# A hybrid decoder layer on one core: the second head pair's q and k are split ahead of the exponentials, and an open projection is closed within the scores

## The chip, the core and the metric

The kernel runs on one core of a Trainium2 chip as one launch. A time is the device time of one execution in microseconds (us); lower is better. Three executions of the kernel before were timed, and one more was taken by the hardware profiler. TensorE (PE in the profile) multiplies matrices, VectorE (DVE) and ScalarE (ACT) work on elements, GpSimd (POOL) does elementwise work and issues DMAs, and SyncE (SP) issues DMAs. Each engine runs its own instructions in the order in which they stand; semaphores hold an instruction until what it needs is done.

## The reference, cut to what matters

One layer on 512 tokens of width 1024, all in float32:

```python
proj = h @ w_in                       # [q | k | v | pool_in | gate_logits]
y_attn = moba_attention(q, k, v, rel_bias) @ w_branch_attn   # 8 heads of 64
y_pool = multiscale_pool(p, w_pool_group, pool_scale) @ w_branch_pool
mixed = gates[:, :, 0] * y_attn + gates[:, :, 1] * y_pool    # gates = sigmoid(g)
h = layer_norm(ALPHA * h + mixed @ w_out, ln1_g, ln1_b)
a, u = split(h @ w_ffn_in)            # 2816 columns each
f = (gelu(causal_dwconv(a)) * u) @ w_ffn_out
h = layer_norm(ALPHA * h + f, ln2_g, ln2_b)
```

With blocks of 256 keys, two blocks in all and up to three chosen, the attention is plain causal softmax attention with a bias by distance:

```python
logits = q @ k.T / 8 + bias[distance]     # masked to the past
p = softmax(logits); out = p @ v
```

## The kernel before, in words

**Precision and form.** Most operands are cut into a high and a low part (`split`, lines 72 to 78): ScalarE rounds the high part into a tile named `whi` or `xT_hi`, and VectorE subtracts to get the low part (`wlo`). A product is then three matmuls, high by high, high by low and low by high (`mm3`, line 245).

**Seven products.** A pair of 128-column weight tiles against 512 tokens is done as a 2 by 2 block product with seven block products in place of eight (`seven`, line 289). Its weight parts are named A, X, D and Y; a group of 12 matmuls 256 wide (`s_mm`) multiplies one half of a part. In order: A twice (banks `sa..` and `sc..`), X, Y (onto the `sa` bank), D (onto the `sb` bank), X's second half (onto `sa`), and last Y's second half (onto `sa`). That last group, with the copy behind it, isn't issued at once: `close` is put in the list `pending`, and `flush` (line 260), called inside the next `seven`, issues it. Between the groups stand small steps: ScalarE copies partial sums out (lines 285, 299, 301), VectorE adds (lines 303, 307, 308). Line 308 writes into the very bank onto which the closing group adds.

**The stages around the change.** v is projected first. Then come five `seven` calls (line 576): number 0 for the pool branch, numbers 1 to 4 for q and k of the four head pairs. In the order of the instructions the bank `sai_674` belongs to the second head pair, `sai_809` to the third, and `sai_999` (after the change: `sai_1011`) to the fourth. `heads_done` (line 523) copies the closed q to the tile `quad`; `split_heads` (line 439) scales and cuts k and q into `kh`, `kl`, `qh`, `ql`. These four tiles exist once (`bufs=1`), so a pair's split has to wait for the last score matmul of the pair before.

**Scores, softmax, PV.** `scores(p)` (line 534) multiplies q and k of the two heads of a pair, 64 rows each, side by side on the two halves of TensorE's rows, into banks `sc0_01`, `sc0_2`, `sc0_3` and so on, and then calls `softmax` per head: VectorE adds the bias strip and takes the maxima (line 561), ScalarE takes the exponentials with their sums (line 567, first of all with a table load), VectorE the reciprocals, GpSimd multiplies (line 572). `trans` (line 618) transposes the result with TensorE; ScalarE copies the first 512 columns of `PT`, VectorE the rest in two copies. `pv` (line 636) multiplies by v in four key blocks, the columns that ScalarE copied first.

**What sets the order.** A scheduler places the instructions of each engine by the order of the code, the dependencies and its own estimates; `issue_after` holds an instruction behind another, `keep_in_program_order` pins it on TensorE. In the code before, the second pair's `split_heads` (line 672) is held behind the maxima and the exponentials of the second head (`nms[1]`, `exps[1]`). The branch and gate weights come through three raw buffers (`wraw`, `araw`) issued by SP, and `weights` fetches up to `state["limit"]`.

Of the kernel before, what the change touches and what calls it, by code (L numbers as in the profile page):

```python
# [18 lines left out]
NT = S // P  # L19
H = 8  # L20
# [32 lines left out]
def layer_kernel(ctx: ExitStack, tc: tile.TileContext, xT, x, w_v, w_c, rel_bias, invcnt, w_group,  # L53
# [30 lines left out]
    at = {}  # L84
# [43 lines left out]
    state = {"next": 0, "limit": WO0 - 1}  # L128
# [310 lines left out]
    def split_heads(p, *behind):  # L439
        qh, ql, kh, kl = QK[p] = [av.tile([P, S], F32R, tag=t, name=f"{t}_{p}", bufs=1)  # L440
                                  for t in ("qh", "ql", "kh", "kl")]
        with ExitStack() as held:
            for ins in behind:
                held.enter_context(tc.issue_after(ins.ins))
            for hi, lo, raw, scale in ((kh, kl, raw_k[p], -1.0), (flip(qh), flip(ql), raw_q[p], DH ** -0.5)):
                nc.scalar.activation(hi, raw, AF.Copy, scale=scale)
                nc.vector.scalar_tensor_tensor(lo, raw, scale, hi.bitcast(F32), op0=ALU.mult, op1=ALU.subtract)
# [79 lines left out]
    Ps = {}  # L527
# [3 lines left out]
    copies = {}  # L531
    offs = [0, P, 3 * P, 6 * P]

    def scores(p):
        two = (2 * p, 2 * p + 1)
        dst = {}
        for h in two:
            if h + 2 < H:
                load_strip(h + 2)
            b01 = bank(f"sc{h}_01")  # L540
            dst[h] = [b01[:, :2 * P], b01[:, 2 * P:], bank(f"sc{h}_2")[:, :3 * P], bank(f"sc{h}_3")]
        qh, ql, kh, kl = QK[p]
        for i in range(NT):
            n = max(2, i + 1) * P
            q = slice(i * P, (i + 1) * P)
            for m, (a, b) in enumerate(((qh, kh), (qh, kl), (ql, kh))):
                for e, h in enumerate(two):
                    own = slice(e * DH, (e + 1) * DH)
                    ins = nc.tensor.matmul(dst[h][i], a[own, q], b[own, :n], start=m == 0, stop=m == 2)
                    if e or m or i:  # L550
                        tc.keep_in_program_order(ins)
        for h in two:
            softmax(h, dst[h])

    def softmax(h, dst):
        pp = aw.tile([P, 10 * P], F32, tag="pp", name=f"pp{h}")
        nm = aw.tile([P, NT], F32, tag="nm", name=f"nm{h}")
        rs = aw.tile([P, NT], F32, tag="rs", name=f"rs{h}")
        for i in range(NT):
            n = (i + 1) * P  # L560
            nc.vector.tensor_tensor_reduce(out=pp[:, offs[i]:offs[i] + n], in0=dst[i][:, :n],
                                           in1=strips[h][:, S - n:], scale=1.0, scalar=-3.0e38,
                                           op0=ALU.add, op1=ALU.max, accum_out=nm[:, i:i + 1])
        nms[h] = nc.vector.tensor_scalar(nm, nm, -1.0, None, op0=ALU.mult)
        for i in range(NT):
            n = (i + 1) * P
            exps[h] = nc.scalar.activation(pp[:, offs[i]:offs[i] + n], pp[:, offs[i]:offs[i] + n], AF.Exp,
                                           bias=nm[:, i:i + 1], accum_out=rs[:, i:i + 1])
        nc.vector.reciprocal(rs, rs)  # L569
        for i in range(NT):  # L570
            n = (i + 1) * P
            state["norm"] = nc.gpsimd.tensor_scalar(pp[:, offs[i]:offs[i] + n], pp[:, offs[i]:offs[i] + n], rs[:, i:i + 1], 1.0,  # L572
                                    op0=ALU.mult, op1=ALU.mult)
        Ps[h] = pp

    for n in range(1 + pairs):
        if n == 0:
            u, done = xr[1][:, 3, :], lambda ba, u: pool_sum(0, ba)
        else:
            u = raw_k[n - 1] = qraw[n - 1][:, S:]  # L580
            done = lambda ba, u, p=n - 1: heads_done(p, ba)
        seven(("i", n), (xT_hi, xT_lo), ti, xr[1][:, 2, n % 2 * 256:n % 2 * 256 + 256], u, done)
        if n == 0:
            behind_sum.close()
            pool_dif(PLAIN[0], state["Y"])
            pool_sum(PLAIN[1], second)
            with tc.issue_after(state["acc"].ins):
                write_table(table)
        elif n == 1:
            pool_out(PLAIN[0])  # L590
            pool_dif(PLAIN[1], state["add"])
            pool_dif(0, state["add"])
            pool_sum(1, xr[1][:, 3, :], -1.0)
            add1 = state["add"]
        elif n == 2:
            pool_out(PLAIN[1])
            pool_dif(1, add1)
            with tc.issue_after(state["acc"].ins):
                load_strip(0)
                load_strip(1)  # L600
            split_heads(0, state["add"], state["copy"])
        elif n == 3:
            pool_out(0)
            pool_out(1)
            pooling.close()
            aw = attn.enter_context(tc.tile_pool(name="aw", bufs=4, side="right", reuse_waits="tile"))
            scores(0)
    phase.close()
    keep = keepp.enter_context(tc.tile_pool(name="keep", bufs=1, reuse_waits="tile"))
    gates = keep.tile([P, H, S], F32, name="gates")  # L610
# [5 lines left out]
    toff = {0: 0, 1: S, 3: S + 3 * P, 2: 2 * S}  # L616

    def trans(h):
        pp = Ps[h]
        PT = ap.tile([P, 10 * P], F32, tag="PT", name=f"PT{h}")  # L620
        bk = [bank(f"tr{h}_{n}") for n in range(3)]
        for kb in (0, 1, 3, 2):
            o = toff[kb]
            for i in range(kb, NT):
                c = o + (i - kb) * P
                nc.tensor.transpose(bk[c // S][:, c % S:c % S + P], pp[:, offs[i] + kb * P:offs[i] + (kb + 1) * P],
                                    ident)
        one = nc.scalar.activation(PT[:, :S], flip(bk[0]), AF.Copy)
        with ExitStack() as held:
            if h + 2 < H:  # L630
                held.enter_context(tc.issue_after(nms[h + 2].ins))
            nc.vector.tensor_copy(PT[:, S:2 * S], flip(bk[1]))
            copies[h] = one, nc.vector.tensor_copy(PT[:, 2 * S:], flip(bk[2][:, :2 * P]))
        PTs[h] = PT

    def pv(p):
        b = bank(f"ob{p}")
        for kb in range(NT):
            n = (NT - kb) * P
            for e in (1, 0):  # L640
                h = 2 * p + e
                state["pv"] = nc.tensor.matmul(b[e * DH:(e + 1) * DH, kb * P:], vv[:, kb, h * DH:(h + 1) * DH],
                                 PTs[h][:, toff[kb]:toff[kb] + n], start=kb == 0, stop=kb == NT - 1)
        split(oT_hi[:, p, :], oT_lo[:, p, :], b)
        state["o"] = state["hi"], state["lo"]

# [22 lines left out]

    with tc.issue_after(exps[0].ins):  # L670
        flush()
    split_heads(1, nms[1], exps[1])
    for h in range(H):
        pair, late = divmod(h, 2)
        if not late and h + 2 < H:
            scores(pair + 1)
        if fill:
            state["limit"] = at["z", 0]
            in_tile(*fill.pop(0))
        elif h < H - 1:  # L680
            early_fetch(h, at["z", 0] + h // 2)
            early_branch(h - 2 * GSEVEN)
        with ExitStack() as held:
            if h and not late:
                pv(pair - 1)
                held.enter_context(tc.issue_after(state["pv"].ins))
            trans(h)
        if not late and h + 4 < H:
            split_heads(pair + 2, nms[h + 3], exps[h + 3])
        if h == 0:  # L690
            with tc.issue_after(nms[2].ins), tc.issue_after(exps[0].ins):
                for k in range(4):
                    split(zT_hi[:, k, :], zT_lo[:, k, :], zT[:, k, :])
            oT_hi = keepz.tile([P, 4, S], F32R, tag="zT", name="oT_hi")
        if h == 5:
            with tc.issue_after(state["norm"].ins):
                for n, (k, t) in enumerate(((k1, t1), (k1, t2), (k2, t1), (k2, t2))):
                    nc.gpsimd.dma_start(quads[n], xT[k.start * P:k.stop * P, t].rearrange("(k p) t -> p k t", p=P))
                homes["g", "X"], homes["g", "D"] = lambda f: gX, lambda f: gD
                for q in "XD":  # L700
                    coming[q].remove(("g", GSEVEN))
                    fetch_raw(("g", GSEVEN), q)
                    homes.pop(("g", q))
        if h == H - 1:
            early_fetch(h, at["o", 1])
            early_branch(h - 2 * GSEVEN)
            state["limit"] = WO0 - 1
# [14 lines left out]
    gx.tile([P, 256], F32, name="gx_gap")  # L722
    for n in parts[1:]:
        tg[n] = tuple(gx.tile([P, 4, 256], F32R, name=f"g{n}_{q}") for q in ("hi", "lo"))
    state["limit"] = WO0 - 1
    mts = {}

# [492 lines left out]
```

## Time and profile before

| what | value |
|---|---|
| median of three executions | 633.39 us (632.47 to 633.95) |
| profiled execution, its own time | 632.73 us |
| span in the profile | 631.0 us |
| mean granted TensorE clock | 0.994 |
| busy: PE, DVE, ACT, POOL | 98%, 81%, 56%, 20% of the span |
| projections of q and k, first two pairs' scores | about 60 to 102 us of the span |
| rest of attention, first branch products | about 102 to 157 us |
| gate products | about 174 to 245 us |

The span is 1.7 us shorter than the time of the same execution, and that execution lies 0.66 us under the median. A line of the timeline reads: start, duration, engine, code line, operation, the tile written and the tiles read, and in brackets how long the engine sat idle before it and what ended that. Matmuls overlap, so what counts for TensorE is the distance from start to start.

### The profile page before, as it was taken

The numbers are of one execution on the slowest core, as the hardware profiler recorded it, in microseconds if no ns is written. First come the engines' busy times: TensorE is split into PE (matmuls) and PEld (weight loads), VectorE is DVE, ScalarE is ACT, GpSimd is POOL, SyncE is SP. The second block draws the span as 40 slices with busy tenths as digits, with TensorE's granted clock in tenths as the row PEclk, the third lists the DMA queues.
The fourth block names the chain that finished last, engine by engine and source line by source line (L and its number), as shares of the span: only waits on it lengthen the run. The fifth ranks groups of instructions, "written<-read, shape, count | busy, mean of one in ns | idle before, by whom it ended". The sixth has DMA issues, their size and how long they took to land.

```text
span 631.0 us, 10674 instructions
## 1 busy us (share of the span) xinstructions
PE 616.8 (98%) x4128; PEld 555.0 (88%) x4128; DVE 508.2 (81%) x793; ACT 354.9 (56%) x541; POOL 125.1 (20%) x133
## 2 busy tenths in 40 slices
PE   9999979999999999999999999999999999999995
PEld 6899868776899999888999999999999888888884
DVE  5978756576869887579998988899888869698886
ACT  6646675463855656306575656666656456555452
POOL 0133133353333111210101011011000302123301
PEclk9999998999999999999999999999999999999998
DMA  8666524019578515624937887777744995899805
GB/s 311 215 190 191 167 67 135 1 35 313 153 200 185 150 35 191 222 122 138 230 129 190 199 194 194 183 192 209 183 118 133 326 272 120 200 203 202 212 1 133
DMA packets 41042, 107.98 MB, mean 171 GB/s; under 512 B 4240, under 2 KB 4760, under 8 KB 40736
## 3 DMA queue, kind: packets, MB, share of 16 engines
q1 hardware_dynamic: 26944, 70.72, 33.0%
q0 software_dynamic: 13472, 35.67, 29.2%
q10 hardware_dynamic: 576, 0.92, 0.4%
q8 instruction: 32, 0.52, 0.3%
q14 instruction: 18, 0.15, 0.1%
HBM read 105.18 MB, written 3.17 MB: 172 GB/s over the span
## 4 chain that ended last, share of the span: by engine, by line
PE 77%; DVE 4%; ACT 2%; DMA 2%; issue 1%; DVEq 0%; ACTq 0%
PE saf L247 4%; PE saf L251 4%; PE saf L250 4%; PE fi L247 3%; PE fi L251 3%; PE fi L250 3%; PE wo L251 2%; PE wo L250 2%; PE wo L247 2%; PE sbf L251 2%; PE sbf L247 2%; PE sbf L250 2%; PE sag L247 2%; PE sag L250 2%; PE sag L251 2%; PE br L247 2%
## 5 line engine op out<-in xcount | busy, mean ns | idle before, releaser
L77 DVE TENSOR_TENSOR wlo<-araw,whi 128x1024 fp32r<-128x1024 f32 x58 | 70.6, 1224 | 7.4 <-ACT whi L76 6.8
L76 ACT ACTIVATE whi<-araw 128x1024 fp32r<-128x1024 f32 x58 | 60.7, 1057 | 24.6 <-PE sag L250 5.1
L77 DVE TENSOR_TENSOR wlo<-wraw,whi 128x1024 fp32r<-128x1024 f32 (+1 forms) x47 | 55.6, 1187 | 16.0 <-ACT whi L76 15.9
L76 ACT ACTIVATE whi<-wraw 128x1024 fp32r<-128x1024 f32 (+1 forms) x47 | 47.6, 1018 | 36.8 <-DMA wraw<-in_w_fo 9.1
L190 POOL DMA_DIRECT2D xraw<-in_w_fi x15 | 18.1, 1204 | 135.5 <-DMA xraw<-in_w_fi 46.2
L76 ACT ACTIVATE whi<-tw 128x1024 fp32r<-128x1024 f32 (+1 forms) x30 | 29.5, 984 | 24.2 <-DMA tw<-in_w_fo 9.7
L77 DVE TENSOR_TENSOR wlo<-tw,whi 128x1024 fp32r<-128x1024 f32 (+1 forms) x30 | 33.4, 1128 | 7.4 <-ACT whi L76 7.4
L247 PE MATMUL saf<-hT_hi,whi 128*128 128x256 f32 x136 | 38.0, 280 | 0.1
L247 PE MATMUL saf<-nT_hi,whi 128*128 128x256 f32 x136 | 38.0, 279 | 0.1
L251 PE MATMUL sbf<-T_hi,wlo 128*128 128x256 f32 x136 | 37.9, 279 | 0.0
L251 PE MATMUL saf<-nT_hi,wlo 128*128 128x256 f32 x136 | 37.8, 278 | 0.0
L250 PE MATMUL saf<-nT_lo,whi 128*128 128x256 f32 x136 | 37.8, 278 | 0.0
L247 PE MATMUL sbf<-T_hi,whi 128*128 128x256 f32 x136 | 37.8, 278 | 0.0
L250 PE MATMUL saf<-hT_lo,whi 128*128 128x256 f32 x136 | 37.7, 278 | 0.0
L250 PE MATMUL sbf<-T_lo,whi 128*128 128x256 f32 x136 | 37.7, 277 | 0.0
L251 PE MATMUL saf<-hT_hi,wlo 128*128 128x256 f32 x136 | 37.7, 278 | 0.0
L250 PE MATMUL fi<-hT_lo,whi 128*128 128x256 f32 (+1 forms) x112 | 36.2, 326 | 0.0
L251 PE MATMUL fi<-hT_hi,wlo 128*128 128x256 f32 (+1 forms) x112 | 36.2, 326 | 0.0
L247 PE MATMUL fi<-hT_hi,whi 128*128 128x256 f32 (+1 forms) x112 | 36.1, 327 | 0.0
L572 POOL TENSOR_SCALAR pp<-pp,rs 128x128 f32<-128x128 f32 (+3 forms) x32 | 23.4, 749 | 24.1 <-DVE rs L569 23.9
L235 POOL DMA_DIRECT2D tw<-in_w_fo x18 | 15.6, 902 | 61.1 <-DVE wlo L77 61.1
L247 PEld LDWEIGHTS saf<-nT_hi,whi 128*128 128x128 f32 x136 | 25.5, 188 | 0.5 <-ACT fT L301 0.3
(359 smaller groups left out, 2218.3 us busy)
## 6 DMA issues: line engine op xcount, KB each, us to landing
tw<-in_w_fo POOLq DMA_DIRECT2D x20, 512.0 KB, 8.2
araw<-in_w_fi SPq DMA_DIRECT2D x17, 512.0 KB, 3.5
xraw<-in_w_fi SPq DMA_DIRECT2D x15, 512.0 KB, 4.2
xraw<-in_w_fi POOLq DMA_DIRECT2D x15, 512.0 KB, 6.6
araw<-in_w_c SPq DMA_DIRECT2D x12, 512.0 KB, 4.4
wraw<-in_w_fi SPq DMA_DIRECT2D x10, 512.0 KB, 3.9
wraw<-in_w_fo SPq DMA_DIRECT2D x10, 512.0 KB, 5.2
tw<-in_w_fo SPq DMA_DIRECT2D x10, 512.0 KB, 7.0
```

What stands on the lines that cost most here:

```text
L76: state["hi"] = nc.scalar.activation(hi, src, AF.Copy)
L77: state["lo"] = nc.vector.tensor_tensor(lo, src, hi.bitcast(F32), op=ALU.subtract)
L190: state["acc"] = nc.gpsimd.dma_start(v, bass.AP(tensor=a.tensor, offset=a.offset, ap=[[pst, pn], [u.offset + S - a.offset, 2], [est, S]]), ...
L235: nc.gpsimd.dma_start(raw, half(then[1:], sl), accum_op=ALU.add)
L247: ins = nc.tensor.matmul(out_, wh, ah, start=start, stop=False, **kw)
L250: nc.tensor.matmul(out_, wh, al, start=False, stop=False, **kw)
L251: nc.tensor.matmul(out_, wl, ah, start=False, stop=stop, **kw)
L572: state["norm"] = nc.gpsimd.tensor_scalar(pp[:, offs[i]:offs[i] + n], pp[:, offs[i]:offs[i] + n], rs[:, i:i + 1], 1.0, op0=ALU.mult, op1=A ...
```

## The change

It does six things.

1. `softmax` is cut in two: `maxima` (bias and maxima, VectorE) stays in `scores`; `softmax` (exponentials, sums, normalising) is called later by the loops.
2. `scores(0)` gets `flush` as `between`: ahead of its last row block the third pair's open projection is closed. Before, that was done inside the fourth pair's `seven`.
3. `split_heads(1)` stands right behind `scores(0)`, ahead of `softmax(0)`, and is held behind nothing but its data. `softmax(1)`, the second head's, stands behind all projections.
4. The three products of a score go `ql kh`, `qh kl`, `qh kh` instead of `qh kh`, `qh kl`, `ql kh`.
5. `pv` takes the key blocks in the order 2, 3, 1, 0, with `start` on the first of these.
6. Behind the last `pv`, the fetch of the weights `("o", 2)` is called by itself, held behind the two copies of the last head.

```diff
-    def scores(p):
+    def scores(p, between=None):
...
         for i in range(NT):
+            if between and i == NT - 1:
+                between()
...
-            for m, (a, b) in enumerate(((qh, kh), (qh, kl), (ql, kh))):
+            for m, (a, b) in enumerate(((ql, kh), (qh, kl), (qh, kh))):
...
         for h in two:
-            softmax(h, dst[h])
-
-    def softmax(h, dst):
+            maxima(h, dst[h])
+
+    def maxima(h, dst):
...
         nms[h] = nc.vector.tensor_scalar(nm, nm, -1.0, None, op0=ALU.mult)
+        Ps[h] = pp, nm, rs
+
+    def softmax(h):
+        pp, nm, rs = Ps[h]
...
-            scores(0)
+            scores(0, flush)
+            split_heads(1)
+            softmax(0)
...
-        pp = Ps[h]
+        pp = Ps[h][0]
...
-        for kb in range(NT):
+        late_first = (2, 3, 1, 0)
+        for kb in late_first:
...
-                                 PTs[h][:, toff[kb]:toff[kb] + n], start=kb == 0, stop=kb == NT - 1)
+                                 PTs[h][:, toff[kb]:toff[kb] + n], start=kb == late_first[0],
+                                 stop=kb == late_first[-1], skip_group_check=True)
...
     with tc.issue_after(exps[0].ins):
         flush()
-    split_heads(1, nms[1], exps[1])
+    softmax(1)
     for h in range(H):
         pair, late = divmod(h, 2)
         if not late and h + 2 < H:
             scores(pair + 1)
+            for n in range(2):
+                softmax(h + 2 + n)
...
+    state["limit"] = at["o", 2]
+    with tc.issue_after(copies[H - 1][0].ins), tc.issue_after(copies[H - 1][1].ins):
+        weights(state["limit"])
     state["limit"] = WO0 - 1
```

**TensorE, the scores of the first pair.** `sai_809` is the third pair's projection, `iT`/`inT` rows are its second half of X, `sc_3` the last row block of the scores. Before, the last score block follows on that half, and then the fourth pair's first group (`sai_999`):

```order
L251 MATMUL sai_809<-inT_hi,wlo_744 128x256
L549 MATMUL sc_3_940<-kh_803,qh_801 128x512
L549 MATMUL sc_3_935<-kl_804,qh_801 128x512
L549 MATMUL sc_3_940<-kl_804,qh_801 128x512
L549 MATMUL sc_3_935<-kh_803,ql_802 128x512
L549 MATMUL sc_3_940<-kh_803,ql_802 128x512
L247 MATMUL sai_999<-xT_hi,whi_856 128x256
```

After, the closing group of the same projection stands right there:

```order
L250 MATMUL sai_809<-inT_lo,whi_743 128x256
L251 MATMUL sai_809<-inT_hi,wlo_744 128x256
L247 MATMUL sai_809<-xT_hi,whi_813 128x256
L250 MATMUL sai_809<-xT_lo,whi_813 128x256
L251 MATMUL sai_809<-xT_hi,wlo_814 128x256
```

The closing group (`xT` rows with `whi_813`) has moved from behind the fourth pair's first 24 matmuls to directly behind the group after which VectorE adds into its bank; the score block follows behind it.

**ScalarE, from the first pair's exponentials to the fourth pair's partial sums.** `pp` are the exponentials, `kh` and `qh` the second pair's split, `whi` weights, `quad_85<-sbi` (line 299) the partial sum on which TensorE's next group of the fourth pair waits. Before:

```order
L567 ACTIVATE pp_982,rs_984<-pp_982,nm_983 128x384
L567 ACTIVATE pp_982,rs_984<-pp_982,nm_983 128x512
L76 ACTIVATE whi_1047<-wraw_1046 128x1024
L446 ACTIVATE kh_1143<-quad_83 128x512
L76 ACTIVATE whi_1066<-wraw_1065 128x1024
L525 ACTIVATE quad_84<-sai_809 128x512
L446 ACTIVATE qh_1141<-quad_83 128x4x128
L299 ACTIVATE quad_85<-sbi_1032 128x256
```

After:

```order
L76 ACTIVATE whi_1046<-wraw_1045 128x1024
L525 ACTIVATE quad_84<-sai_809 128x512
L446 ACTIVATE kh_996<-quad_83 128x512
L446 ACTIVATE qh_994<-quad_83 128x4x128
L285 ACTIVATE xr_107<-sai_1011 128x256
L76 ACTIVATE whi_1065<-wraw_1064 128x1024
L573 ACT_TABLE_LOAD
L573 ACTIVATE pp_978,rs_980<-pp_978,nm_979 128x128
L573 ACTIVATE pp_978,rs_980<-pp_978,nm_979 128x256
L573 ACTIVATE pp_978,rs_980<-pp_978,nm_979 128x384
L573 ACTIVATE pp_978,rs_980<-pp_978,nm_979 128x512
L299 ACTIVATE quad_85<-sbi_1044 128x256
```

The split has moved ahead of the table load and of all eight exponentials; four of these now stand ahead of the copy of line 299, and the other four (the second head's) ahead of that of line 301.

**ScalarE, the last heads.** `PT_1656` and `PT_1673` are the transposed weights of heads 6 and 7, `whi_1751` the last branch weights. Before:

```order
L76 ACTIVATE whi_1697<-wraw_1696 128x1024
L76 ACTIVATE oT_hi<-ob_1645 128x512
L76 ACTIVATE whi_1751<-wraw_1750 128x1024
L628 ACTIVATE PT_1656<-tr_0_1657 128x512
L628 ACTIVATE PT_1673<-tr_0_1674 128x512
```

After:

```order
L76 ACTIVATE whi_1697<-wraw_1696 128x1024
L76 ACTIVATE oT_hi<-ob_1645 128x512
L635 ACTIVATE PT_1656<-tr_0_1657 128x512
L635 ACTIVATE PT_1673<-tr_0_1674 128x512
L76 ACTIVATE whi_1751<-wraw_1750 128x1024
```

The two copies have moved ahead of the weight cut, which waits for a transfer.

More of the change, by code (lines that the diff above doesn't have):

```diff
@@ L573, in softmax @@
                                     op0=ALU.mult, op1=ALU.mult)
-        Ps[h] = pp
     for n in range(1 + pairs):
```

## The prediction

> **What bounds the kernel now.** I begin with the busy table and the waits of TensorE:
>
> ```profile
> PE 616.8 (98%) x4128; PEld 555.0 (88%) x4128; DVE 508.2 (81%) x793; ACT 354.9 (56%) x541; POOL 125.1 (20%) x133
> PE sc L549 <- ACT qh L446: 4.9, 1, 4.9
> PE ob L642 <- ACT PT L628: 0.3, 1, 0.3
> ```
>
> TensorE is busy for 98% of the span, so only two things shorten the program: less matmul work, or less waiting on TensorE. The change removes no matmul. Of the waits, one stands out: the second pair's scores wait 4.9 us, once, for ScalarE's `qh`. The chain of work that ended last shows what ScalarE did meanwhile:
>
> ```profile
> 90.66 0.71 ACT pp L567 x2
> 91.37 0.94 ACT whi L76
> 92.31 0.52 ACT kh L446
> 92.83 0.95 ACT whi L76
> 93.78 0.48 ACT quad L525
> 94.26 0.53 ACT qh L446
> 94.83 0.80 PE sc L549 x4
> ```
>
> Exponentials first, then two weight cuts and a copy, with `kh` and `qh` in between, where line 672 holds them. TensorE's timeline around it, and two windows:
>
> ```profile
> 89.68 0.28 PE L251 MATMUL sai<-inT_hi,wlo 128*128 128x256 f32 x1
> 94.83 0.58 PE L549 MATMUL sc<-kh,qh 64*128 64x256 f32 x2 [4.87 <-ACT qh L446]
> 95.56 0.58 PE L247 MATMUL sbi<-iT_hi,whi 128*128 128x256 f32 x1
> 98.28 0.28 PE L247 MATMUL sai<-inT_hi,whi 128*128 128x256 f32 x1
> ...
> 95.00:100.00 5.00, 5.00 (x32) 4.64 (x34) 2.19 (x4) 1.96 (x5) 1.69 (x1) 0.67 0.58 197
> 150.00:154.00 4.00, 3.69 (x16) 2.12 (x15) 2.72 (x4) 2.03 (x3) 0.00 (x0) 1.00 1.03 381
> ```
>
> The gap costs twice. After 4.87 us idle, the granted clock (third number from the end) is 0.67 over the next 5 us, so 5 x 0.33 = 1.6 us more are lost. The 0.3 us wait at 152 us leaves it at 1.00.
>
> **The change part by part.** *Split ahead of the exponentials.* TensorE's cover for the split is what stands between the two pairs' scores. After the change that is the fourth pair's groups A (24 matmuls), X (12) and Y (12). Between 80.48 and 81.65 (rows below) lie 10 steps of this width, 0.117 us each, so the cover is 48 x 0.117 = 5.6 us. The work under it:
>
> ```profile
> L77 DVE TENSOR_TENSOR wlo<-wraw,whi 128x1024 fp32r<-128x1024 f32 (+1 forms) x47 | 55.6, 1187 | 16.0 <-ACT whi L76 15.9
> 83.00 0.68 DVE L561 CUSTOM_DVE_ANT_0 pp<-sc,strip 128x512 f32<-128x512 f32 x1
> 128.27 0.99 DVE L447 SCALAR_TENSOR_TENSOR ql<-quad,qh 128x512 fp32r<-128x512 f32 x1
> ```
>
> The tiles exist once, so `kh` starts behind the last score matmul; `kh` and `qh` take 0.52 + 0.53 us on ScalarE. VectorE's queue holds, ahead of `kl` and `ql`, at worst one weight cut (1.19) and the two last maxima (2 x 0.68); with two halves at most 0.99 each that makes 4.5 us. It fits in 5.6. So the 4.87 goes, and with it the 1.6 of slow clock: **-6.5**.
>
> *The closed projection.* Here a new wait is made. The closing group adds onto the bank that VectorE writes at line 308, and it now stands directly behind the group that VectorE waits for; before, the score block and 24 matmuls of the fourth pair stood between.
>
> ```profile
> 79.93 0.39 PE L549 MATMUL sc<-kh,qh 64*128 64x512 f32 x1
> 80.25 0.39 PE L247 MATMUL sai<-inT_hi,whi 128*128 128x256 f32 x1
> 80.48 0.28 PE L250 MATMUL sai<-inT_lo,whi 128*128 128x256 f32 x1
> 81.65 0.28 PE L251 MATMUL sai<-inT_hi,wlo 128*128 128x256 f32 x1
> 82.66 0.43 DVE L308 TENSOR_TENSOR sai<-xr,sci 128x256 f32<-128x256 f32 x1
> ```
>
> Before, line 308 ends at 82.66 + 0.43 = 83.09, and TensorE could have gone on at 81.65 + 0.12 = 81.77: 1.32 us. The lone score pass ahead of the group (0.32, from 79.93 to 80.25) moves behind it, so TensorE comes earlier still, VectorE doesn't: **+1.6**. Behind the wait stand the closing group, the score block and, on ScalarE, the weight cut `whi_1046` that needs the closing group's end. No row shows this wait. Bounds: 1.0 if VectorE comes earlier by as much as the score blocks ahead of it shrink, 2.2 if its six maxima come 0.6 later because two heads' scores now end in one block. I take 1.6, from the nearest rows.
>
> Fewer score blocks: one block less among the projections of the first pair. A block of one pair of matmuls cost
>
> ```profile
> 75.55 0.28 PE L250 MATMUL sai<-inT_lo,whi 128*128 128x256 f32 x1
> 75.76 0.39 PE L549 MATMUL sc<-kl,qh 64*128 64x256 f32 x2
> 76.30 0.28 PE L250 MATMUL sbi<-iT_lo,whi 128*128 128x256 f32 x1
> ```
>
> 0.75 us for three steps instead of 0.35, so 0.4 for entering and leaving half-height rows; **-0.3** (0 to 0.4), since such a cost varies from block to block.
>
> *Exponentials behind the split.* The table load and the first head's four exponentials now stand ahead of the copy of line 299, for which the fourth pair's group D waits:
>
> ```profile
> 85.60 1.28 ACT L567 ACT_TABLE_LOAD   x1 [0.76 <-DVE nm L564]
> 86.90 0.40 ACT L567 ACTIVATE pp<-pp,nm 128x128 f32<-128x128 f32 x1
> 89.09 0.39 ACT L567 ACTIVATE pp<-pp,nm 128x128 f32<-128x128 f32 x1
> 94.68 0.37 ACT L299 ACTIVATE quad<-sbi 128x256 f32<-128x256 f32 x1
> 94.95 0.37 ACT L301 ACTIVATE quad<-sai 128x256 f32<-128x256 f32 x1
> ```
>
> Count from TensorE's restart R at the closing group. TensorE, a score pass counted by its width (0.117 per 256 columns) and 0.2 added per block: 12 matmuls 1.4, the score block of three 512-wide passes 0.9, 48 matmuls 5.6, the second pair's first 19 scores (six passes 256 wide, three 384, one 512) 1.7: at D by R + 9.6. ScalarE: the cut `whi_1065` needs the buffer that the end of A frees, R + 1.4 + 0.9 + 2.8 = R + 5.1, and with 0.1 allowed for the signal and 0.95 for itself ends at R + 6.15; table load to first exponential 1.30; four exponentials 86.90 to 89.09, 2.19; line 299 to 301, 0.27: R + 9.9, with the signal R + 10.05. **+0.45** (0 to 1.2, if the maxima hold the table load longer). The second head's four (2.2) stand ahead of line 301, but TensorE has D, scores and ten 512-wide matmuls before it needs that; nothing waits. GpSimd's normalising comes later by these steps, but the transposes stand behind 24 matmuls 512 wide. No DMA moves past another except in the gate products, where nothing waited.
>
> *Low part first.* The first score matmul now needs `ql`, the last of the split. For the fourth pair, `ql` is ready at 128.27 + 0.99 = 129.26, and TensorE comes at 128.85, the first row here; the others belong to the next step:
>
> ```profile
> 128.85 0.39 PE L549 MATMUL sc<-kh,qh 64*128 64x256 f32 x2
> 116.86 0.41 DVE L633 COPY PT<-tr 128x256 f32<-128x256 f32 x1
> 121.46 2.38 PE L642 MATMUL ob<-PT,vv 128*64 128x512 f32 x16
> 130.98 0.41 DVE L633 COPY PT<-tr 128x256 f32<-128x256 f32 x1
> 134.34 2.37 PE L642 MATMUL ob<-PT,vv 128*64 128x512 f32 x16
> 144.42 0.41 DVE L633 COPY PT<-tr 128x256 f32<-128x256 f32 x1
> 144.49 2.37 PE L642 MATMUL ob<-PT,vv 128*64 128x512 f32 x16
> 150.18 1.06 ACT L76 ACTIVATE whi<-wraw 128x1024 fp32r<-128x1024 f32 x1 [2.67 <-DMA wraw<-in_w_br]
> ```
>
> So 0.4 later, of which the third product lost a part before: **+0.2** (0 to 0.4).
>
> *PV and the last weights.* `pv` now starts with block 2, VectorE's second copy. In the rows above that copy ends 4.2 us ahead of the first PV (117.27 against 121.46) and 3 us ahead of the second, but for the third it ends at 144.83, when TensorE is free at about 144.4: **+0.4** (0 to 0.8). Ahead of the fourth, ScalarE's cut of the last branch weights had waited 2.67 us for its transfer with `PT` behind it; that cut now stands behind the copies, and the 0.31 wait goes: **-0.3**.
>
> Sum: -6.5 + 1.6 - 0.3 + 0.45 + 0.2 + 0.4 - 0.3 = -4.4 us. The profiled execution took 632.73 us (span 631.0 and 1.7 around it), so 628.3; the median of the runs shown is 633.39, 0.66 above it, and by that 629.0. That is the number I forecast. From 102 us on the rest is shifted as a whole, transfers too, since they are issued when TensorE's, VectorE's or ScalarE's steps free their buffers.
>
> **The rivals.** *The new wait closes the clock too.* The 4.87 gap did; 0.31 did not; 1.6 lies between, and a second short wait follows it. If it does, 1.6 us come back: 630.6. For it: nothing in this trace shows the length at which it begins. Against it: 1.6 is nearer to 0.31 than to 4.87. [...] Chance 0.12.
>
> *The new waits don't come.* VectorE may come to line 308 earlier than I count, and the score blocks may hide line 299. Then 633.39 - 6.5 - 0.3 - 0.3 = 626.3. Against it: line 308 needs the end of the group directly ahead, so some wait is left. Chance 0.12.
>
> *The wait only moves.* The 4.9 us in which ScalarE does exponentials are then spent by TensorE at line 299 or 301: within 0.2%, about 633.2. The order shows the split ahead of them, so it does what it says; but if the maxima come 3 to 4 us later than I count, this is what happens. Chance 0.06.
>
> *Slower.* Same place, one mechanism: the table load waits for the maxima and stands ahead of four exponentials and line 299. Each us by which it is late beyond R + 6.15 is a us of wait at D. [...] At R + 11.2, 5 us late, the sum is -4.4 + 5 + 1.6 = +2.2: 635.6. Against it: before, the maxima released the table load at 85.60, 2.5 us behind the end of line 308 (83.09); the count here leaves them 6.15. Chance 0.04.
>
> **How the numbers follow.** Forecast 0.66, early 0.12, clock 0.12, moved 0.06, slower 0.04. The forecast's own range, its costs moved to one end one or two at a time, is 627.5 to 630.2. To leave out no more than 2 in 10, the range reaches from 626.3, where no new wait comes, to 630.9, the clock case with 0.3 of an unknown cost on top; the last two cases are outside. About 0.2%, 1.27 us, is what a measurement of this kernel can tell from no change: 0.90 for faster (first three cases), 0.06 for the same, 0.04 for slower.
>
> **What would show it.** In the changed profile: no wait of the second pair's scores on `qh` or `ql`, a clock of 1.00 around 90 to 100 us; a wait of 1 to 2 us of `sai` (closing group) on VectorE's line 308 near 81 to 83 us; one under 1.2 us of `sbi` on ScalarE's line 299 near 92 us; a short one of `ob` on VectorE in the third PV. I am wrong if the closing group's wait is over 2.5 us, if the clock falls behind it, or if a wait over 1 us appears after 102 us.

## The result, and the profile after

| | before | after |
|---|---|---|
| median of the timed executions | 633.52 us (632.47 to 633.95, four) | 627.28 us (626.77 to 627.78, four) |
| profiled execution, its own time | 632.73 us | 627.43 us |
| its span and mean granted clock | 631.0 us, 0.994 | 625.7 us, 0.998 |

The ratio of the medians is 0.9904, with a 95% interval of 0.9887 to 0.9921. The forecast was 629.0 us, in a range of 626.3 to 630.9: the sign was right, the number 1.7 us too high.

The busy table and TensorE's waits in the profile after, but for two at the program's start that the kernel before has too (1.2 us of the warm-up, 0.2 on the first weights); the columns of the list are the total, how often, and the longest:

```profile
PE 614.3 (98%) x4128; PEld 553.3 (88%) x4128; DVE 511.1 (82%) x793; ACT 355.1 (57%) x541; POOL 116.0 (19%) x133
PE sai L247 <- DVE sai L308: 1.4, 1, 1.4
PE sc L551 <- DVE ql L447: 0.5, 1, 0.5
PE sbi L247 <- ACT quad L299: 0.5, 1, 0.5
PE ob L650 <- DVE PT L640: 0.2, 1, 0.2
```

The 4.9 us on `qh` are gone, and four small waits have come, at the four places that the prediction named. TensorE's and ScalarE's rows at the first two, and the windows from 85 to 95 us, with the granted clock as the third number from the end:

```profile
80.85 0.28 PE L251 MATMUL sai<-inT_hi,wlo 128*128 128x256 f32 x1
82.56 0.39 PE L247 MATMUL sai<-xT_hi,whi 128*128 128x256 f32 x1 [1.43 <-DVE sai L308]
90.81 0.39 PE L551 MATMUL sc<-kh,ql 64*128 64x256 f32 x2
93.02 0.39 PE L247 MATMUL sbi<-iT_hi,whi 128*128 128x256 f32 x1 [0.47 <-ACT quad L299]
```

```profile
89.11 1.28 ACT L573 ACT_TABLE_LOAD   x1
92.60 0.36 ACT L299 ACTIVATE quad<-sbi 128x256 f32<-128x256 f32 x1
```

```profile
85.00:90.00 5.00, 5.00 (x44) 4.95 (x43) 4.67 (x10) 4.10 (x7) 1.08 (x2) 1.00 0.67 228
90.00:95.00 5.00, 4.53 (x43) 3.84 (x42) 2.62 (x14) 4.99 (x18) 1.91 (x4) 1.00 0.55 179
```

The closing group waits 1.43 us for line 308; from start to start that is 82.56 - 80.85 - 0.12 = 1.59 us lost. The second pair's scores at 90.81 wait for nothing. The copy of line 299 ends behind the table load and four exponentials, and group D loses 0.47. The granted clock stays at 1.00 behind both.

The stage by which the kernels are compared below runs from the last of the pool matmuls `zb`, which stand ahead of the change's place, to the first score of the third pair, behind it. Its two ends, before and then after:

```profile
72.67 1.02 PE L481 MATMUL zb<-pw,wg 128*128 128x512 f32 x2
116.36 0.39 PE L549 MATMUL sc<-kh,qh 64*128 64x256 f32 x2
```

```profile
72.48 1.02 PE L481 MATMUL zb<-pw,wg 128*128 128x512 f32 x2
111.64 0.39 PE L551 MATMUL sc<-kh,ql 64*128 64x256 f32 x2
```

43.69 us against 39.16: 4.53 of the 5.3 us between the two spans lie in this stage.

### The profile page after: what moved, and what is told of

Read it like the earlier page. It is cut to its first block, busy times and chain, and to the rows that moved or that the text cites. A ratio compares the mean times of both kernels' runs of the same rounds, so it can differ in the third digit from the quotient of the medians.

```text
span 625.7 us, 10679 instructions
## 1 busy us (share of the span) xinstructions
PE 614.3 (98%) x4128; PEld 553.3 (88%) x4128; DVE 511.1 (82%) x793; ACT 355.1 (57%) x541; POOL 116.0 (19%) x133
## 4 chain that ended last, share of the span: by engine, by line
PE 76%; DVE 4%; ACT 2%; DMA 2%; issue 1%; DVEq 0%; ACTq 0%; SPq 0%; POOLq 0%
PE saf L247 5%; PE saf L251 5%; PE saf L250 4%; PE fi L247 3%; PE fi L250 3%; PE fi L251 3%; PE wo L250 2%; PE wo L247 2%; PE wo L251 2%; PE sbf L251 2%; PE sbf L247 2%; PE sbf L250 2%; PE sag L247 2%; PE sag L250 2%; PE sag L251 2%; PE foa L247 2%
## 5 line engine op out<-in xcount | busy, mean ns | idle before, releaser
L77 DVE TENSOR_TENSOR wlo<-araw,whi 128x1024 fp32r<-128x1024 f32 x58 | 71.9, 1247 | 9.4 <-ACT whi L76 8.9
L578 POOL TENSOR_SCALAR pp<-pp,rs 128x128 f32<-128x128 f32 (+3 forms) x32 | 21.8, 699 | 26.5 <-DVE rs L575 18.6
L247 PEld LDWEIGHTS saf<-hT_hi,whi 128*128 128x128 f32 x136 | 25.5, 188 | 0.3 <-DVE saf L308 0.3
```

The lines of the kernel that those rows point to most:

```text
L77: state["lo"] = nc.vector.tensor_tensor(lo, src, hi.bitcast(F32), op=ALU.subtract)
L247: ins = nc.tensor.matmul(out_, wh, ah, start=start, stop=False, **kw)
```

## The experiments

Each ratio is to the kernel before, run beside it on the same chip. "Stage" is the stretch just defined, in the profiled execution; "clock" is the mean granted clock of each execution. Two kernels that were executed once each, with idle times of 2.90 and 1.77 us, stand in the text alone.

| run | median us | ratio, 95% interval | stage us | clock |
|---|---|---|---|---|
| the changed kernel again | 627.16 | 0.9889 (0.9868 to 0.9909) | 39.18 | 0.996 to 0.998 |
| no early closing | 630.02 | 0.9947 (0.9923 to 0.9970) | 41.27 | 0.990 to 0.995 |
| old place of the split | 633.96 | 0.9999 (0.9980 to 1.0018) | 45.10 | 0.990 to 0.993 |
| the split alone | 632.01 | 0.9976 (0.9961 to 0.9990) | 43.41 | 0.991 to 0.997 |
| old product order and fetch | 628.93 | 0.9928 (0.9905 to 0.9950) | 39.17 | 0.996 to 0.998 |
| old order of the score products | 627.75 | 0.9902 (0.9876 to 0.9928) | 39.58 | 0.996 to 0.998 |
| idle of 1.64 us | 627.47 | 0.9921 (0.9891 to 0.9951) | 39.37 | 0.996 to 0.998 |
| idle of 1.77 us, again | 628.73 | 0.9929 (0.9914 to 0.9943) | 41.03 | 0.993 to 0.998 |
| closing behind the scores | 626.00 | 0.9869 (0.9845 to 0.9892) | 37.94 | 0.997 to 0.998 |
| and the reciprocal later | 624.64 | 0.9852 (0.9824 to 0.9881) | 37.02 | 0.996 to 0.998 |

My theory was that of the prediction: the split ahead of the exponentials removes the wait on `qh` and the slow clock behind it, everything else is small change. The rivals: the early closing or the later parts carry the gain; the new wait closes the clock as well.

**The changed kernel again**, as a reference on one chip with three others.

> The changed kernel itself, unchanged, for comparison on the same chip with the three kernels beside it. Both theories: 627.3 us, ratio to the kernel before 0.990, the same waits as before (1.4 on line 308, 0.5 on line 299, 0.5 on `ql`).

Measured 627.16 us (626.82 to 627.76), with the same waits and a stage of 39.18: both theories had it.

**The split back in its old place.**

```diff
             scores(0, flush)
-            split_heads(1)
             softmax(0)
...
     softmax(1)
+    split_heads(1, nms[1], exps[1])
```

> Nothing is left out. The changed kernel with only the place of the second pair's split undone: it stands behind the second head's exponentials again, the early closing, the new score order and the new order of the attention-value product are kept. ScalarE then does table load, eight exponentials and a weight cut, 6 to 7 us, ahead of `kh` and `qh`, and the copy of line 299 stands behind these. My theory: TensorE waits 4 to 5 us once in front of the fourth pair's group D or the second pair's scores, the granted clock falls to about 0.67 behind it, and the time is 632 to 633.5, near that of the kernel before. Rival (the closing, the merged blocks and the later parts carry the gain): under 630, clock at 1.00.

Measured 633.96 us, half a microsecond above the range, on a chip where the kernel before took 634.19. The largest wait of TensorE, ScalarE's rows ahead of its end, and two windows:

```profile
PE sbi L247 <- ACT quad L299: 5.2, 1, 5.2
```

```profile
87.76 1.28 ACT L573 ACT_TABLE_LOAD   x1 [0.85 <-DVE nm L566]
94.38 0.61 ACT L446 ACTIVATE kh<-quad 128x512 fp32r<-128x512 f32 x1
95.42 0.36 ACT L299 ACTIVATE quad<-sbi 128x256 f32<-128x256 f32 x1
```

```profile
90.00:95.00 5.00, 0.64 (x6) 0.44 (x4) 1.68 (x3) 5.00 (x16) 3.25 (x5) 0.77 0.27 87
95.00:100.00 5.00, 4.17 (x21) 4.17 (x22) 2.00 (x4) 2.42 (x5) 2.81 (x4) 0.55 0.25 93
```

ScalarE is busy for all of 90 to 95 us, `kh` and line 299 come behind it, and the wait and the slow clock are back, now in front of group D. Everything but the place of the split was kept, and nothing is left of the gain. My theory holds in this: without the split there is none.

**No early closing.**

```diff
-            scores(0, flush)
+            scores(0)
             split_heads(1)
```

> Nothing is left out of the computation. The third pair's projection is not closed within the first pair's scores; its closing group stands behind the fourth pair's first 24 matmuls again, and 60 matmuls instead of 48 lie between the two pairs' scores. My theory (the gain is the removed wait on `qh` and the clock behind it, and the early closing by itself costs 1.6 us): the 1.4 us wait on line 308 goes, the second pair's scores still wait for nothing, and since line 299 now stands behind two heads' exponentials the fourth pair's group D waits 0.5 us, at most 1.5. Time 626.0 us, 1.3 below the changed kernel. Rival (the early closing is what frees the split: the weight cut and the copies behind it come too late otherwise): a wait on `qh` or `ql` of 1 us or more is back and the time is 629 or more.

Measured 630.02 us, so I was wrong: 2.7 above the changed kernel's 627.28 (another set of runs), not 1.3 below it. The rival's time came, but not by its wait on `qh`. The second pair's last score block, row by row, and the row of ScalarE that released its first matmul:

```profile
92.11 0.49 PE L551 MATMUL sc<-kh,ql 64*128 64x512 f32 x1 [1.67 <-ACT quad L525]
93.41 0.74 PE L551 MATMUL sc<-kh,ql 64*128 64x512 f32 x1 [0.81 <-DVE nm L563]
```

```profile
91.49 0.57 ACT L525 ACTIVATE quad<-sai 128x512 f32<-128x512 f32 x1
```

The block has its `q` and `k` (`ql` was done at 85.7 us) but no bank to write to. The eight banks of `ps` are taken by the projections still open and by the scores; the copy of line 525, which empties the third pair's closed bank, stands behind seven of the eight exponentials. The sum agrees with the stage: the waits on line 308 (1.59) and line 299 (0.47) go, 1.67 and 0.81 come, and a slow stretch of 3.4 us (93.4 to 96.8 us in TensorE's rows; the granted clock is 0.84 from 90 to 95 us and 0.81 from 95 to 100) costs (0.16 + 0.19) x 5 = 1.7: -2.06 + 2.48 + 1.7 = +2.12, against 41.27 - 39.16 = 2.11, closer than the terms are exact. So the early closing isn't only a cost of 1.6: its copy gives a bank back in time.

**The split alone**, the kernel before with `softmax` cut in two and this edit:

```diff
             scores(0)
+            split_heads(1)
+            softmax(0)
...
-    split_heads(1, nms[1], exps[1])
+    softmax(1)
```

> Nothing is left out. The kernel before with one part of the change alone: the second pair is split ahead of the exponentials, and the exponentials are taken out of the maxima's function. No early closing, the old order of the score products and of the attention-value product, no held fetch. My theory (the early closing serves to give a bank back to the second pair's last score blocks; without it those wait for ScalarE's copy behind the exponentials): the wait on `qh` goes, waits of 2 to 3.5 us on line 525 and the maxima come at the second pair's last score block, with a clock under 0.9 behind them: 629.5 to 631.5, 2.5 to 4 below the kernel before. Rival (the split alone carries the whole gain): 627.5 or less.

Measured 632.01 us, half a microsecond above the range that I gave. The waits were those expected, the clock behind them was worse:

```profile
93.10 0.50 PE L551 MATMUL sc<-kh,qh 64*128 64x512 f32 x1 [1.95 <-ACT quad L525]
94.40 0.76 PE L551 MATMUL sc<-kh,qh 64*128 64x512 f32 x1 [0.80 <-DVE nm L563]
```

```profile
95.00:100.00 5.00, 5.00 (x24) 4.35 (x21) 3.03 (x13) 1.26 (x3) 3.13 (x6) 0.50 0.37 122
100.00:105.00 5.00, 5.00 (x24) 4.34 (x24) 2.44 (x6) 5.00 (x18) 2.57 (x6) 0.90 0.50 179
```

1.95 + 0.80 of waiting, and 2.5 + 0.5 us lost to the clock from 95 to 105 us: 5.75, against 4.87 + 1.6 before. The row at 94.40, 0.76 us long where the one ahead takes 0.50, is slow already, so some 0.3 more is lost ahead of 95 us; with it 6.05 against 6.47, where the stage is 0.28 us shorter. The split alone gains 0.24% (0.10% to 0.39%), the closing and the later parts without the split nothing (the old place of the split, above), all of it together 1.0%. Split and closing each remove a wait that the other leaves standing.

**The old order of the attention-value product, and no held fetch.**

```diff
-        late_first = (2, 3, 1, 0)
-        for kb in late_first:
+        for kb in range(NT):
...
-    state["limit"] = at["o", 2]
-    with tc.issue_after(copies[H - 1][0].ins), tc.issue_after(copies[H - 1][1].ins):
-        weights(state["limit"])
```

> Nothing is left out. The changed kernel with the key blocks of the attention-value product in the old order 0, 1, 2, 3 and without the held fetch of the last branch weights. My theory: this part is worth 0.15 to 0.3 us, the fourth product waits 0.3 us for ScalarE's `PT` again and the third loses its 0.16, so 627.4, not to be told from the changed kernel. Rival (the gain above what I counted, 5.3 in the profiles against 4.4, comes from here): 628.0 or more, and the fourth product in two pieces again.

Measured 628.93 us, on a chip whose times spread more (627.40 to 631.09), so the interval of its ratio overlaps that of the changed kernel. The profiles say more. The fourth product, and ScalarE ahead of it, in this kernel:

```profile
147.88 1.08 PE L649 MATMUL ob<-PT,vv 128*64 128x512 f32 x4 [0.61 <-ACT PT L635]
152.06 1.51 PE L649 MATMUL ob<-PT,vv 128*64 128x384 f32 x12
```

```profile
145.80 1.06 ACT L76 ACTIVATE whi<-wraw 128x1024 fp32r<-128x1024 f32 x1 [2.97 <-DMA wraw<-in_w_br]
146.76 1.06 ACT L635 ACTIVATE PT<-tr 128x512 f32<-128x512 f32 x2
```

and in the changed kernel:

```profile
147.56 2.37 PE L650 MATMUL ob<-PT,vv 128*64 128x256 f32 x16
```

The copies of `PT` stand behind a cut that waits 2.97 us for its transfer; the product waits 0.61 and comes in two pieces. From the stage's start to the first `wo` matmul this kernel takes 173.56 us, the changed one 172.73: the part is worth 0.8 us there, what the rival expected and not my 0.15 to 0.3. The run undoes the order and the held fetch together, so their shares stay open. From there to the end the same two profiles differ by 0.7 the other way, a stretch that varied by 0.9 among all profiles here (379.8 to 380.7), so the spans don't show it.

**The old order of the score products.**

```diff
-            for m, (a, b) in enumerate(((ql, kh), (qh, kl), (qh, kh))):
+            for m, (a, b) in enumerate(((qh, kh), (qh, kl), (ql, kh))):
```

> Nothing is left out. The changed kernel with the three products of a score block in the old order, so that the first matmul needs `qh` and `kh` and not `ql`. My theory: the fourth pair's wait on `ql` (0.49) goes, all else stays, so 0.3 to 0.5 below the changed kernel. Rival (the new order belongs to the early split): a wait of the second pair's scores on `kl` or `ql`, and no gain or a loss.

Measured 627.75 us: no gain, so my 0.3 to 0.5 didn't come; nor did the rival's wait. The first pair's first score row, then the fourth pair's score block and the first row behind it, with the old order:

```profile
75.14 0.39 PE L551 MATMUL sc<-kh,qh 64*128 64x256 f32 x2
126.25 0.39 PE L551 MATMUL sc<-kh,qh 64*128 64x256 f32 x2
128.82 0.50 PE L247 MATMUL br<-zT_hi,whi 128*128 128x512 f32 x1
```

and with the new:

```profile
124.69 0.39 PE L551 MATMUL sc<-kh,ql 64*128 64x256 f32 x2 [0.49 <-DVE ql L447]
126.82 0.50 PE L247 MATMUL br<-zT_hi,whi 128*128 128x512 f32 x1
```

The fourth pair's block takes 2.57 us in the old order, 2.13 in the new. What the first matmul doesn't wait (0.49) is for the most part lost inside the block (0.44). At the start of the stage the order does more. In the old order the scheduler places the first pair's first product in a score block of its own (75.14), as in the kernel before; in the new one it stands with the second product, and TensorE enters one block less. With the old order the stage is 0.42 us longer (39.58 against 39.16). Behind the stage the two kernels agree, since the third attention-value product then waits 0.32 us in place of 0.16: 133.57 us each to the first `wo` matmul. So by the profiles this part is worth some 0.4 us; the times (627.75 and 627.16, with overlapping intervals of the ratio) can't tell that from nothing.

**A longer idle in front of the closing group.** Three kernels make VectorE multiply by 1.0 at line 308. The first does so behind it, on the bank, with a weight cut in between:

```diff
         state["add"] = nc.vector.tensor_tensor(ba[:, t1], y, c11, op=ALU.add)
+        if key == ("i", 3):
+            for _ in range(1):
+                nc.vector.tensor_scalar(ba[:, t1], ba[:, t1], 1.0, None, op0=ALU.mult)
```

> Nothing is left out: the bank of line 308 is multiplied once by 1.0 ahead of the closing group, behind a weight cut that VectorE does first. TensorE's idle time in front of the closing group grows from 1.43 to about 2.95 us. My theory (the clock falls only behind a longer idle, between 2.95 and 4.87): granted clock 1.00 in the 5 us behind it, time 1.5 above the changed kernel, 628.9. Rival (an idle of this length already closes the clock): a clock of 0.67 to 0.9 behind it, and 630 or more.

```profile
85.45 0.39 PE L247 MATMUL sai<-xT_hi,whi 128*128 128x256 f32 x1 [2.90 <-DVE sai L311]
86.84 0.33 PE L251 MATMUL sai<-xT_hi,wlo 128*128 128x256 f32 x1
90.34 0.28 PE L250 MATMUL sai<-xT_lo,whi 128*128 128x256 f32 x1
...
85.00:90.00 5.00, 4.55 (x24) 3.62 (x25) 2.22 (x6) 2.69 (x4) 0.00 (x0) 0.69 0.33 105
```

The idle is 2.90 us, the clock falls to 0.69, the stage is 3.3 us longer (1.5 of idle, 1.8 of clock) and the one execution took 631.51 us. The rival was right. The second kernel multiplies a block of 512 between lines 307 and 308, held there with `issue_after`:

```diff
-        nc.vector.tensor_tensor(u[:, t2], u[:, t2], chain, op=ALU.add)
+        held = ExitStack()
+        before_ = nc.vector.tensor_tensor(u[:, t2], u[:, t2], chain, op=ALU.add)
+        if key == ("i", 3):
+            for _ in range(1):
+                held.enter_context(tc.issue_after(before_.ins))
+                before_ = nc.vector.tensor_scalar(u, u, 1.0, None, op0=ALU.mult)
+            held.enter_context(tc.issue_after(before_.ins))
         state["add"] = nc.vector.tensor_tensor(ba[:, t1], y, c11, op=ALU.add)
+        held.close()
```

> Nothing is left out: VectorE multiplies a 512-wide row block by 1.0 between lines 307 and 308, so that TensorE's idle time in front of the closing group grows from 1.43 to about 2.05 us; the order of all else is that of the changed kernel. Theory A (any idle of 2 us closes the clock, as 2.90 did): granted clock of 0.7 to 0.9 in the 5 us behind it and 1.5 to 2.2 above the changed kernel in the profile. Theory B (2 us are too short): clock 1.00 and 0.6 above it. I hold B for somewhat more likely, since 1.43 with 0.47 ten us later left the clock at 1.00, and 1.67 with 0.81 behind it lowered it only to 0.81 to 0.84.

```profile
82.93 0.39 PE L247 MATMUL sai<-xT_hi,whi 128*128 128x256 f32 x1 [1.77 <-DVE sai L314]
83.97 0.28 PE L251 MATMUL sai<-xT_hi,wlo 128*128 128x256 f32 x1
84.22 0.42 PE L250 MATMUL sai<-xT_lo,whi 128*128 128x256 f32 x1
87.59 0.28 PE L251 MATMUL sai<-xT_hi,wlo 128*128 128x256 f32 x1
```

The idle is 1.77, shorter than I had counted, and still the matmuls slow down (0.42 where 0.28 is usual), from about 84.1 to 87.5 us. The granted clock is 0.92 from 80 to 85 us and 0.74 from 85 to 90: (0.08 + 0.26) x 5 = 1.7 us lost in those 3.4, half of them. The stage is 1.83 us longer, the one execution took 628.94. Theory A (that 2 us suffice) was right, where I had leant to B. Then the same kernel again, and one with a block of 256 (`y` in place of `u`):

> The kernel of the 2 us gap again (its idle time in front of the closing group was 1.77 us), for the granted clock of each of several executions. [...] Theory B (what counts is the length of one idle stretch, with a limit between 1.45 and 1.77): every execution at about 0.994 and near 628.9.

> Nothing is left out: as the 2 us gap, but with a row block of 256 instead of 512 multiplied by 1.0, so an idle time of about 1.6 us in front of the closing group, by the 0.34 that the wider multiply added. [...] Theory B (a limit on one idle stretch between 1.45 and 1.77): all executions alike, at 0.996 to 0.998 or at 0.994.

The first row in each, and a window behind the second's; the second of the three rows is where the slow stretch of the 1.77 us kernel begins this time:

```profile
82.58 0.39 PE L247 MATMUL sai<-xT_hi,whi 128*128 128x256 f32 x1 [1.77 <-DVE sai L314]
83.09 0.41 PE L247 MATMUL sai<-xT_hi,whi 128*128 128x256 f32 x1
86.61 0.39 PE L247 MATMUL sai<-xT_hi,whi 128*128 128x256 f32 x1
```

```profile
82.55 0.39 PE L247 MATMUL sai<-xT_hi,whi 128*128 128x256 f32 x1 [1.64 <-DVE sai L314]
...
85.00:90.00 5.00, 5.00 (x44) 4.96 (x43) 4.69 (x10) 4.10 (x7) 1.08 (x2) 1.00 0.71 234
```

After 1.64 us the mean clock was 0.996 to 0.998 in all four executions and the stage 0.21 us longer, the idle alone. (One of the four took 632.05 us at a clock of 0.998; no run shows why.) After 1.77 us it was 0.993 to 0.995 in five of six and 0.998 in the sixth, whose time (628.34 us) is however no shorter than the others' (628.26 to 629.75). The slow stretch begins 0.5 us behind the restart here and 1.2 in the run above, and is 3.4 us long in both. By theory B, a limit on a single idle stretch, the six should be alike. The one that differs in its clock, without the gain in time, doesn't settle that, and no run shows what sets the start of the slow stretch.

**The closing behind the scores.** Two runs follow from the ones above: get rid of the wait on line 308, and keep the bank's early return.

```diff
-            scores(0, flush)
+            scores(0)
+            flush()
             split_heads(1)
-            softmax(0)
+            with tc.issue_after(state["copy"].ins):
+                softmax(0)
```

> Nothing is left out. The closing group is called behind all of the first pair's scores instead of within them, and the first head's exponentials are held behind the closed projection's copy of line 525, so that the copy gives its bank back early. My theory (the early closing is worth having only because its copy frees a bank for the second pair's last score block, and its price is the wait on line 308): that wait (1.4, 1.6 from start to start) goes, the one on line 299 goes too, since 17 gate matmuls now stand ahead of group D; a wait of 0.3 to 0.8 us of the second pair's last score block on VectorE's maxima comes. Clock 1.00 from 80 to 100 us. Time 1.2 to 1.8 below the changed kernel, about 625.8. Rival (the closing has to stand within the scores): a wait on line 525 of over 1 us as in the run without the closing, a clock under 0.9, and 628 or more.

Measured 626.00 us beside 627.16 for the changed kernel on the same chip; the intervals of the two ratios overlap, so the stage has to show the gain. Line 308 and line 299 are gone from the waits; what came, and why, in two rows of TensorE and VectorE:

```profile
93.44 0.46 PE L551 MATMUL sc<-kh,ql 64*128 64x512 f32 x1 [0.99 <-DVE nm L563]
```

```profile
92.53 0.18 DVE L575 RECIPROCAL rs<-rs 128x4 f32<-128x4 f32 x1 [2.87 <-ACT pp L573]
```

Stage: -1.59 - 0.47 + 0.99 = -1.07, measured 37.94 - 39.16 = -1.22. The closing group stands among the fourth pair's first matmuls again, but the copy of line 525 is ahead of the exponentials, and the wait on that copy doesn't come: it was the copy's place that mattered. The last score block now waits for a bank that VectorE's maxima give back, and VectorE sits 2.87 us in front of a reciprocal that waits for the exponentials.

**And that reciprocal later**, with the edits of the run before; `mx` is the instruction that takes a row block's maxima, so the first head's reciprocal and multiplies stand behind the second block of head 3:

```diff
+            if (h, i) == (3, 1):
+                first_max.append(mx)
...
+        if h:
+            normal(h)
+
+    def normal(h):
+        pp, nm, rs = Ps[h]
         nc.vector.reciprocal(rs, rs)
...
             scores(pair + 1)
+            if not h:
+                with tc.issue_after(first_max[0].ins):
+                    normal(0)
```

> Nothing is left out. The kernel with the closing group behind the first pair's scores and the copy of line 525 ahead of the exponentials, and in addition the first head's reciprocal behind the second pair's first maxima on VectorE, since it stood in front of them there and waited for the exponentials. My theory (the 0.99 us wait of the second pair's last score block was that of the reciprocal): the wait goes or falls under 0.2 us, and the time falls by 0.8 to 1.0 below that kernel's ratio of 0.987, to about 0.9855 of the kernel before, some 625. Rival (the last block waits for the maxima themselves): a wait of 0.5 us or more stays, and the ratio stays near 0.987.

Measured 624.64 us (624.16 to 625.26), ratio 0.9852. No listed wait of TensorE between 76 and 120 us is left; its list, but for 0.5 us on the transfer of the first weights:

```profile
PE warm_ps L346 <- DVE warm L343: 1.2, 1, 1.2
PE sc L552 <- DVE ql L447: 0.5, 1, 0.5
PE ob L660 <- DVE PT L650: 0.2, 1, 0.2
```

The stage is 2.14 us shorter than the changed kernel's, about what the two waits in it make (1.59 + 0.47). All its executions lie under the changed kernel's shortest (626.77). The interval of its ratio (0.9824 to 0.9881) lies below that of the changed kernel's first result (0.9887 to 0.9921) and touches that of its second (0.9868 to 0.9909). It is a version that beats both.

## Why the prediction was right, and where it was off

- **The split ahead (-6.5).** Right: the wait and the slow clock went, and with the split in its old place both came back, the wait at 5.2 us. But the step "It fits in 5.6. So the 4.87 goes" counted only whether `kh` to `ql` are ready in time. It left out the banks: without the early closing the same scores lose 1.67 and 0.81 us and a slow stretch for want of one. The number came out right by luck: another part of the change, which I had priced as a cost, met a condition that I hadn't seen.
- **The closed projection (+1.6).** Its wait was 1.43 us, 1.59 from start to start. Right in size, but priced as a cost alone; its other side is the bank.
- **Fewer score blocks (-0.3) and line 299 (+0.45).** The wait on line 299 was 0.47. The block is gone, but what removed it is the order of the products, which I had priced at +0.2 alone: the run with the old order has the block back, at 0.4 us. All terms of the stage together were forecast at -6.5 + 1.6 - 0.3 + 0.45 = -4.75; it was -4.53.
- **Score order (+0.2).** A wait of 0.49 came, over the bound of 0.4, and most of it is there with the old order too, spread inside the block. From the start of the transposes ahead (122.94 us, and 125.07 in the run with the old order) to the end of the block it is 3.88 us against 3.75, a cost of 0.13. With the score block that it saves (the point above), the order is a gain and not a cost.
- **The third and fourth PV (+0.4 and -0.3).** This is the term that was mis-sized. The third waits 0.16, and from the branch matmuls ahead of it to its start it is 0.2 longer than in the kernel before (3.15 against 2.92). The fourth gained more than its wait: kept in one piece it saves the second entry as well (2.37 us against 1.08 + 1.51), and from the branch matmuls ahead of it (148.95 us before, 144.62 after) to the first `wo` matmul it is 0.8 shorter (100.59 against 101.36). That makes some -0.5 us, not +0.1. Against the old order on top of all else the part is worth -0.8, since the fourth's wait has there grown to 0.61.
- **The profile's frame.** 0.2 us of the spans' difference lie ahead of the stage, 0.2 behind `wo`, both without a part in the change. Forecast 628.3 in that frame, measured 627.43. Of the 0.9, some 0.6 is the PV term and 0.4 these two ends; the stage, 0.2 short of its forecast, takes part of that back.
- **The median's frame.** The medians differ by 6.2 us, the profiled executions by 5.3. The mean clock of 55 executions of the kernel before that ran beside the experiments was 0.990 to 0.995, with a median of 0.992 to 0.994 in each set, and that of the changed kernel 0.996 to 0.998. The profiled 0.994 was some 0.001 above their middle, and 0.001 of 631 us is 0.6. I had added 0.66 to the forecast, as for a shift that both kernels share; the changed kernel's profiled execution lies 0.15 above its median instead. That the varying slow clock of the kernel before is the cause is argued, not shown.
- **The clock rival (0.12).** It didn't happen at 1.43 us, but "1.6 is nearer to 0.31 than to 4.87" was no argument: behind 1.77 us it fell, to 0.74 from 85 to 90 us. The new wait is 0.34 us short of that one, which cost 1.5 us on top of itself.

## What to carry to other kernels

When an operand is made ready earlier, look for the next thing that its consumer needs, the bank it writes to first of all, and which copy on which engine gives that bank back. Two edits that each remove one of several waits in front of the same instruction can be worth little or nothing alone and much more together, so they are to be priced together. Where TensorE must wait a little, one wait of up to 1.64 us cost here no more than itself, and one of 1.77 cost 1.5 us on top. Whether short waits add up isn't settled; since 1.67 and 0.81 us within 3 us did lower the clock (0.84 and 0.81 in the two windows), keeping the sum of waits that close together under 1.6 is my estimate, from these two and the 1.64 that left it at 1.00. And treat an instruction that waits for another engine (the reciprocal that sat 2.87 us for the exponentials, the weight cut that sat 2.97 for its transfer) as a wait of all that is queued behind it.

## What the runs showed of the hardware

The granted clock falls after much shorter idle times than I had thought. 1.43 to 1.45 us left it at 1.00 in each profile that had it, and so did 1.64. It fell behind 1.77 us in both profiles (0.92 and 0.74 in the windows from 80 to 85 and 85 to 90 us of the first, 0.80 and 0.86 in those of the second) and behind 1.67 and 0.81 us within 3 us (0.84 from 90 to 95 us, 0.81 from 95 to 100). Where both ends of a slow stretch can be seen (behind 1.77, 1.77 and 2.90 us) it was 3.4 us long, so it cost 1.5 to 1.8 us at each of these idle times, and it began 0.5 to 1.4 us after the work had started again. With the split alone the granted clock was 0.50 from 95 to 100 us and the matmuls were slow up to 101.2 us, 6.8 us after the second wait had ended, which is twice the 3.4. What decides when the clock falls, and for how long, isn't shown by these runs beyond these lengths.
